# Expert weight ring with its xT slots last, p in a tile of its own, gate and up of the last 512 columns packed side by side, and a nested second fallback, in a two-layer decoder trunk

## The chip, the cores and the metric

The kernel runs on one core of one Trainium2 chip. The metric is device time in microseconds, the median of three runs. Five engines work side by side: TensorE (PE, its weight loads PEld), VectorE (DVE), ScalarE (ACT), GpSimd (POOL) and SyncE (SP); SP issues nearly all DMAs here, in order.

## The reference

A batch of one sequence of 256 tokens of width 1024 goes through two layers in float32. Layer 0 is forgetting and stick-breaking attention and a dense SwiGLU; layer 1 is sliding-window attention and a mixture of experts. What matters here is the mixture and what follows it:

```python
def moe_swiglu(x, router_w, router_b, w_gate_up, w_down):
    logits = jnp.einsum('td,de->te', xf, router_w) + router_b
    top_v, top_i = lax.top_k(logits, TOP_K)                    # 2 of 8 experts
    gates = jax.nn.softmax(top_v, axis=-1)
    ...
    for e in range(N_EXPERTS):                                 # swiglu: (silu(g) * u) @ w_down
        y = y + combine[:, e:e + 1] * swiglu(xf, w_gate_up[e], w_down[e])
...
x = layer_norm(DEEPNORM_ALPHA * x + h, ln_ffn_g[i], ln_ffn_b[i])
x = x + jax.nn.sigmoid(x @ ple_w_gate[i]) * (p[i] @ ple_w_proj[i])
```

An expert has 1024x3584 gate weights, as many up weights and 3584x1024 down weights. All eight are read: 336 tiles of 1 MiB.

## The kernel before

**Stages.** Layer 0 and the attention of layer 1 come first (up to about 464 us). Then come the router, the eight experts, and the end (layer norm, the gated embedding, the output). The experts run in an order sorted by their token counts, which the chip works out. GR gives each place in that order 3 or 2 groups of 32 tokens (3, 2, 3, 3, 2, 3, 3, 2). If some expert has more tokens than its place holds, a fallback runs all experts again for the rest: `experts(1, ...)`, and `experts(2, ...)` for still more. Both are compiled in, behind two tests one after the other (lines 1338 to 1341). With this input neither body runs.

**An expert.** An expert is cut in four quarters of the hidden width: 1024 columns three times, then 512. `gate_up(e, q)` multiplies the gathered tokens `xg` by gate and up weights. `trans(e, q)` transposes the product h, `down(e, q)` multiplies it by the down weights. The program goes gate_up(e, q), down of the quarter before, trans(e, q). `side_by_side` (line 1074) splits a weight row block in four strips and issues four matmuls for each group of 32 tokens, each into its own 32 PSUM partitions (a quarter of the array's columns). A T.matmul in float32 is two instructions in the trace.

For q below 3 the block is 1024 columns of gate, then 1024 of up, so the strips are 256 wide. For q = 3 the 1 MiB tile holds two k steps, each of 512 gate and 512 up columns. These are two blocks of 512 (lines 1096 and 1097), whose strips are 128 wide: as many matmuls as in another quarter, half as wide.

**The ring.** Weights go through 22 slots of 1 MiB, `ringtile` (line 787), in the cyclic order of TURNS (line 120). A digit or letter 0 to c is a slot of the ring pool, "p" one of 7 `raw` tiles, "x" one of two `xT` tiles. A tile's load waits until the tile 22 places before it has been read, and loads are issued in order (`fetch_`, line 830). The first AHEAD = 16 tiles, gate_up(0, 0) and gate_up(0, 1), are requested ahead of the router (line 853). The 17th to the 20th are the four of down(0, 0), then come those of gate_up(0, 2). In TURNS the two x stand at places 17 and 18, the slots 9, a, b, c after them.

The tag `xT` has two buffers. The router uses both for a transposed x (`xTf`, line 859). Then `pt1` (line 891), which holds p of layer 1 until `turn_p` (line 1211) has transposed it on TensorE, takes the first of them again, so the two x tiles get the second and, behind pt1, the first. `turn_p` is issued behind gate_up(0, 0) in the program; a scheduler sets each engine's static order.

**The end.** `Finish.load` and `Finish.prepare` take 21 further ring tiles after gate_up(7, 3): loads of 6 MiB, and weights split in high and low parts. down(7, 2), down(7, 3) and `Finish.end` follow.

Of the kernel before, what the change touches and what calls it, by code (L numbers as in the profile page):

```python
# [11 lines left out]
F32 = mybir.dt.float32  # L12
# [3 lines left out]
AF = mybir.ActivationFunctionType  # L16
ALU = mybir.AluOpType
AX = mybir.AxisListType

P = 128  # L20
S = 256
D = 1024
NB = S // P
# [14 lines left out]
CT = 32  # L38
# [36 lines left out]
def trunk(ctx: ExitStack, tc: tile.TileContext, cst, x, p, ln_mix_g, ln_mix_b, ln_ffn_g, ln_ffn_b, ab_w_in,  # L75
# [29 lines left out]
    V, A, T, G = (Engine(eng) for eng in (nc.vector, nc.scalar, nc.tensor, nc.gpsimd))  # L105

    def pool(name, bufs=1, **kw):
        return tc.tile_pool(name=name, bufs=bufs, **kw)

    cp = ctx.enter_context(pool("cp"))  # L110
    big = ctx.enter_context(pool("big"))
# [5 lines left out]
    HLW = 1024  # L117
    TMB = 1
    RB = 13
    TURNS = "3p4p5p6p7ppp2108xx9abc"  # L120
    KT = 2
    SC = (0, 2, 5)
    NLAST = (256, 256)
# [2 lines left out]
    def acc():  # L126
        return psA.tile([P, 512], F32, tag="acc", name="acc")

    def mis():
        return psM.tile([P, 512], F32, tag="mis", name="mis")  # L130
# [30 lines left out]
    ident = c[:, C_ID:C_ID + P]  # L161
# [16 lines left out]
    def gemm(hl, lhs, nk, w, col0, width, accs, seg=4, kh=2, korder=None, loaded=None, raws=None):  # L178
# [7 lines left out]
        for k0, kn in segs:  # L186
# [19 lines left out]
            for b in range(NB):  # L206
# [3 lines left out]
                for k in range(k0, k0 + kn):  # L210
                    H, L = parts[k]
                    for j, (a, W) in enumerate(((0, H), (0, L), (1, H))):
                        T.matmul(accs[b][:, :width], lhs(b, a, k), W,
                                 start=(k == 0 and j == 0), stop=(k == nk - 1 and j == 2))
# [13 lines left out]
    def tr4(src, n=4):  # L228
        ps = mis()
        for i in range(n):  # L230
            turned[0] = T.transpose(ps[:, i * P:(i + 1) * P], src[:, i * P:(i + 1) * P], ident)
        return ps

    def xTtile():
        return big.tile([P, 2, 8, P], F32R, tag="xT", name="xT", bufs=2)
# [12 lines left out]
    def lnp(g_ap, b_ap):  # L248
        g = big.tile([P, D], F32, tag="lng", name="lng", bufs=1)
        bt = big.tile([P, D], F32, tag="lnb", name="lnb", bufs=1)  # L250
        nc.sync.dma_start(g, g_ap.broadcast_to([P, D]))
        nc.sync.dma_start(bt, b_ap.broadcast_to([P, D]))
        return g, bt
# [65 lines left out]
    def to_xT(tiles):  # L319
        r = []  # L320
        for b in range(NB):
            t = xTtile()
            tsplit(tiles[b], t)
            r.append(t)
        return r
# [88 lines left out]
    xT = [xTtile()]  # L414
# [15 lines left out]
    with pool("hl0", 5, side="right") as hl, ExitStack() as es0:  # L430
# [160 lines left out]
        g, bt = lnp(ln_mix_g[0:1, :], ln_mix_b[0:1, :])  # L591
        order = [4, 5, 6, 7, 0, 1, 2, 3]
        accs = gemm_full(hl, lambda b, a, k: oT[:, a, order[k], b * P:(b + 1) * P], 8, ab_w_out[0], korder=order)
        xT = [xTtile() for b in range(NB)]
# [68 lines left out]
        with pool("ff", 1, reuse_waits="tile") as ff:  # L663
            hTs = []
            for f0 in range(0, DFF, 512):
                w = min(512, DFF - f0)
# [5 lines left out]
                hT = ff.tile([P, 2, 4, S], F32R, tag="hT", name="hT", bufs=6)  # L672
                hTs.append(hT)
                for b in range(NB):
                    h = ff.tile([P, 512], F32, tag="h", name="h", bufs=2)
# [3 lines left out]
            g, bt = lnp(ln_ffn_g[0:1, :], ln_ffn_b[0:1, :])  # L679
# [8 lines left out]
        with pool("pl", 1, reuse_waits="tile") as pl:  # L688
            xT = to_xT(xs)
# [7 lines left out]
        with pool("at1", 1, reuse_waits="tile") as at:  # L697
            xT = to_xT(xs)
# [27 lines left out]
            for b in range(NB):  # L726
# [6 lines left out]
                ps = tr4(kd.rearrange("p g r d -> p (g r d)"), 2)  # L733
# [38 lines left out]
            g, bt = lnp(ln_mix_g[1:2, :], ln_mix_b[1:2, :])  # L772
# [4 lines left out]
        moe = ctx.enter_context(pool("moe", 1, reuse_waits="tile"))  # L777
# [9 lines left out]
    def ringtile(dt=F32):  # L787

        i = TURNS[turn[0] % len(TURNS)]
        turn[0] += 1  # L790
        if i == "p":
            return rawtile(dt)
        if i == "x":
            return big.tile([P, 2048], dt, tag="xT", name="raw", bufs=2)
        return ring.tile([P, 2048], dt, tag="raw" + i, name="raw", bufs=1)
# [32 lines left out]
    chunks = [(c_.stop - c_.start) // P for c_ in cols]  # L828
# [24 lines left out]
    for i in range(AHEAD):  # L853
        t = ringtile()
# [3 lines left out]
    for b in range(NB):  # L858
        t = big.tile([P, 2, 8, P], F32, tag="xT", name="xTf", bufs=2)
        for k0 in range(0, 8, 4):  # L860
            ps = tr4(xs[b][:, k0 * P:(k0 + 4) * P])
            A.copy(t[:, 0, k0:k0 + 4, :], ps.rearrange("p (k t) -> p k t", t=P))
        ps = mis()
        for k in range(8):
            q = T.matmul(ps[0:NE, 0:P], rw[:, k, :], t[:, 0, k, :], start=(k == 0), stop=(k == 7))
# [3 lines left out]
    for b in range(NB):  # L869
        ps = lps[b]  # L870
# [13 lines left out]
        ps = mis()  # L884
# [3 lines left out]
        place_first(b)  # L888
        gather_first(b)

    pt1 = big.tile([P, NB, 256], F32, tag="xT", name="pt1", bufs=2)
    nc.sync.dma_start(pt1, p[1, 0].rearrange("(b p) n -> p b n", p=P))
    accx = xs

# [88 lines left out]
    def experts(rest, finish):  # L983

        st = {}
# [11 lines left out]
        used, passed = [0], [None]  # L997
# [24 lines left out]
        def weights(*it):  # L1022
            assert items[used[0]] == it
            used[0] += 1
            return fetch(*it)
# [47 lines left out]

        def side_by_side(out, lhs, W, first, last):

            w = W.shape[-1] // 4
            for g, (o, opens) in enumerate(out):
                for t in range(4):
                    mm = T.matmul(o[CT * t:CT * (t + 1), :w], lhs[g], W[:, w * t:w * (t + 1)],
                                  start=first and opens, stop=last, skip_group_check=True)  # L1080
            return mm

        def gate_up(e, q, hooks={}):
            xg = st[e]["xg"]
            n = gr[e]
            w = 32 * chunks[q]
            ac = [acc() for _ in range(n)]

            out = [[(ac[s][:, :w], True), (ac[s][:, w:2 * w], False)] + [(a[:, w * s:w * (s + 1)], s == 0) for a in ac[2:]]
                   for s in range(2)]  # L1090
            for k in range(8):
                lhs = [xg[:, k, CT * g:CT * (g + 1)] for g in range(n)]
                if q < 3:
                    W = [weights(e, q, k, s) for s in range(2)]
                else:
                    t = weights(e, q, k, 0)
                    W = [t[:, :512], t[:, 512:]]
                for s in range(2):
                    mm = side_by_side(out[s], lhs, W[s], k == 0, k == 7)
                if k in hooks:  # L1100
                    hooks[k](mm)
            h = moe.tile([P, 3 * 256], F32, tag="h", name="h", bufs=1)
            A.activation(h[:, :2 * w], ac[0][:, :2 * w], AF.Silu)
            V.tensor_tensor(h[:, :2 * w], h[:, :2 * w], ac[1][:, :2 * w], op=ALU.mult)
            if n > 2:
                A.activation(h[:, 2 * w:3 * w], ac[2][:, :w], AF.Silu)
                V.tensor_tensor(h[:, 2 * w:3 * w], h[:, 2 * w:3 * w], ac[2][:, w:2 * w], op=ALU.mult)
            st[e]["h%d" % q] = h

        def trans(e, q):  # L1110

            m = chunks[q] // 4
            n = gr[e] * m
            hT = moe.tile([P, 6, 4, CT], F32, tag="hT", name="hT", bufs=1)
            with tc.issue_after(passed[0].ins) if passed[0] else nullcontext():
                for i in range(0, n, 4):
                    j = min(4, n - i)
                    ps = tr4(st[e]["h%d" % q][:, i * P:(i + j) * P], j)
                    A.copy(hT[:, i:i + j].rearrange("p j t i -> p (j t i)"), ps[:, :j * P])
            st[e]["hT%d" % q] = hT  # L1120

        def down(e, q):
            n = gr[e]
            m = chunks[q] // 4
            if q == 0:
                st[e]["y"] = [mis() for _ in range((n + 1) // 2)]
            y = [(st[e]["y"][g // 2][:, 256 * (g % 2):256 * (g % 2 + 1)], g % 2 == 0) for g in range(n)]
            hT = st[e]["hT%d" % q]
            for k in range(chunks[q]):
                W = weights(e, q, k)  # L1130
                mm = side_by_side(y, [hT[:, g * m + k % m, k // m, :] for g in range(n)], W,
                                  q == 0 and k == 0, q == 3 and k == chunks[3] - 1)
                if k == min(KT, chunks[q] - 1):
                    passed[0] = mm
# [8 lines left out]
        def ystile():  # L1143
            return moe.tile([P, D], F32, tag="ys", name="ys", bufs=1)
# [38 lines left out]
        for e in range(NE):  # L1183
            for q in range(4):
# [17 lines left out]
                if e == NE - 1 and q == 3:  # L1202
                    scatter(e)[0](None)
        down(NE - 1, 3)
        ys = ystile()
        finish.end(functools.partial(collect, st[NE - 1]["y"], ys, gr[NE - 1]), ys, st[NE - 1]["pT"], CT * gr[NE - 1],
# [8 lines left out]
    class Finish:  # L1215
# [41 lines left out]
        def end(self, collect, ys, pT, c_, add):  # L1257
# [33 lines left out]
            with in_order():  # L1291
# [38 lines left out]
                for m in NLAST:  # L1330
# [3 lines left out]
                    c0 += m  # L1334

    experts(0, Finish())

    top = nc.values_load(cnti[0:1, 0:1], min_val=0, max_val=S + P)
    for rest in range(1, 3):
        with tc.If(top > P + 3 * CT * (rest - 1)):  # L1340
            experts(rest, Finish())


_INS = ['x', 'p', 'ln_mix_g', 'ln_mix_b', 'ln_ffn_g', 'ln_ffn_b', 'ab_w_in', 'ab_b_f', 'ab_w_out', 'c_w_qkv',
# [19 lines left out]
```

## Time and profile before

| what | value |
|---|---|
| median of 3 runs | 1430.46 us (1430.26 to 1434.83) |
| the profiled execution | 1428.27 us |
| its span, first to last instruction | 1426.5 us |
| TensorE busy | 1358.0 us (95%) |
| VectorE, ScalarE busy | 394.1 us, 325.2 us |
| moved by DMA | 434.03 MB, mean 304 GB/s |
| mean granted TensorE clock | 0.99 |

The profile is of one execution. Its span leaves out 1.77 us of its time. Ends of matmuls are modelled, so that a busy TensorE says little by itself; the duration of a phase is better read from its start to the start of the next.

### The profile page before, as it was taken

The numbers are of one execution on the slowest core, as the hardware profiler recorded it, in microseconds if no ns is written. First come the engines' busy times: TensorE is split into PE (matmuls) and PEld (weight loads), VectorE is DVE, ScalarE is ACT, GpSimd is POOL, SyncE is SP. The second block draws the span as 40 slices with busy tenths as digits, with TensorE's granted clock in tenths as the row PEclk, the third lists the DMA queues.
The fourth block names the chain that finished last, engine by engine and source line by source line (L and its number), as shares of the span: only waits on it lengthen the run. The fifth ranks groups of instructions, "written<-read, shape, count | busy, mean of one in ns | idle before, by whom it ended". The sixth has DMA issues, their size and how long they took to land. (4 is left out here: it accounts for less than half of the span.)

```text
span 1426.5 us, 40108 instructions
## 1 busy us (share of the span) xinstructions
PE 1358.0 (95%) x18290; PEld 927.4 (65%) x18290; DVE 394.1 (28%) x781; ACT 325.2 (23%) x618; POOL 27.5 (2%) x31
## 2 busy tenths in 40 slices
PE   8999899999999999898999899899999899999886
PEld 6786688887876666555556655665655665665545
DVE  5465755556676400010010010001010001001152
ACT  4545444434574101010010010010010001001131
POOL 0000200000000000000000000000000000000000
PEclk9999999999999999999999999999999999999988
DMA  9362553664573259999999999999999999999941
GB/s 323 142 209 78 185 178 118 206 207 166 204 287 118 98 223 401 407 408 401 407 408 391 406 408 391 403 408 396 396 408 403 390 408 407 387 406 407 359 186 35
DMA packets 143166, 434.03 MB, mean 304 GB/s; under 512 B 8834, under 2 KB 14978, under 8 KB 142978
## 3 DMA queue, kind: packets, MB, share of 16 engines
q1 hardware_dynamic: 142834, 431.22, 79.4%
q8 instruction: 147, 2.41, 0.7%
q14 instruction: 41, 0.34, 0.1%
q10 hardware_dynamic: 144, 0.07, 0.0%
HBM read 430.21 MB, written 1.05 MB: 302 GB/s over the span
## 5 line engine op out<-in xcount | busy, mean ns | idle before, releaser
L90 PE MATMUL acc<-raw,xg 128*32 128x256 f32 (+1 forms) x10752 | 528.5, 355 | 27.0 <-issue 23.1
L90 PEld LDWEIGHTS acc<-raw,xg 128*32 128x32 f32 x10752 | 333.4, 111 | 216.2 <-issue 41.0
L90 PE MATMUL mis<-raw,hT 128*32 128x256 f32 x4704 | 265.2, 379 | 7.1 <-DMA raw<-in_moe_w_down 4.0
L90 PE MATMUL acc<-H,xT 128*128 128x512 f32 (+2 forms) x768 | 226.1, 378 | 2.2 <-DVE xT L90 1.3
L90 PEld LDWEIGHTS mis<-raw,hT 128*32 128x32 f32 x4704 | 154.9, 110 | 107.4 <-issue 8.0
L90 DVE TENSOR_TENSOR h<-h,acc 128x512 f32<-128x512 f32 (+1 forms) x64 | 35.3, 552 | 681.3 <-PE acc L90 679.6
L90 DVE TENSOR_TENSOR L<-raw,H 128x1024 fp32r<-128x1024 f32 (+2 forms) x134 | 151.2, 1134 | 115.4 <-ACT H L90 114.7
L90 ACT CAST H<-raw 128x1024 fp32r<-128x1024 f32 (+2 forms) x138 | 133.6, 975 | 150.3 <-PE acc L90 144.3
L90 PEld LDWEIGHTS acc<-H,xT 128*128 128x128 f32 x768 | 139.4, 190 | 30.4 <-ACT xT L90 1.8
L90 ACT ACTIVATE h<-acc 128x512 f32<-128x512 f32 (+1 forms) x64 | 31.3, 489 | 515.0 <-PE acc L90 514.9
L90 PE MATMUL acc<-L,xT 128*128 128x512 f32 (+2 forms) x384 | 141.8, 375 | 0.0
L90 PEld LDWEIGHTS acc<-L,xT 128*128 128x128 f32 x384 | 72.7, 189 | 14.0 <-DVE L L90 1.2
L90 ACT COPY hT<-mis 128x512 f32<-128x512 f32 (+2 forms) x47 | 21.7, 495 | 202.2 <-PE mis L90 202.0
L90 PE MATMUL acc<-H,hT 128*128 128x512 f32 x176 | 55.8, 396 | 0.0
L90 DVE SCALAR_TENSOR_TENSOR x<-mis,gateT,x 128x512 f32<-128x512 f32 x28 | 21.0, 751 | 92.4 <-PE mis L90 90.9
L90 PE MATMUL acc<-H,oT 128*128 128x512 f32 x128 | 44.4, 413 | 0.0
L90 PEld LDWEIGHTS acc<-H,hT 128*128 128x128 f32 x176 | 33.0, 187 | 8.0
L90 PE MATMUL acc<-L,hT 128*128 128x512 f32 x88 | 34.8, 395 | 0.0
L90 DVE COPY ys<-mis 32x256 f32<-32x256 f32 x42 | 17.8, 423 | 49.9 <-ACT ys L90 42.0
L90 PEld LDWEIGHTS mis<-c,h 128*128 128x128 f32 x191 | 20.9, 140 | 13.6 <-issue 11.9
L90 PE MATMUL mis<-c,h 128*128 128x128 f32 x191 | 29.7, 281 | 0.0
L90 PEld LDWEIGHTS acc<-H,oT 128*128 128x128 f32 x128 | 24.0, 189 | 6.0 <-issue 0.8
(209 smaller groups left out, 792.2 us busy)
## 6 DMA issues: line engine op xcount, KB each, us to landing
raw<-in_moe_w_gate_up SPq DMA_DIRECT2D x192, 1024.0 KB, 18.4
raw<-in_moe_w_down SPq DMA_DIRECT2D x111, 1024.0 KB, 18.4
raw<-in_moe_w_gate_up SPq DMA_DIRECT2D x64, 512.0 KB, 13.3
raw<-in_ffn_w_gate_up SPq DMA_DIRECT2D x20, 1024.0 KB, 5.1
raw<-in_ffn_w_down SPq DMA_DIRECT2D x10, 1024.0 KB, 5.1
raw<-in_ab_w_in SPq DMA_DIRECT2D x9, 1024.0 KB, 8.0
raw<-in_ple_w_gate SPq DMA_DIRECT2D x8, 1024.0 KB, 13.3
raw<-in_ab_w_out SPq DMA_DIRECT2D x4, 1024.0 KB, 5.1
```

Of the source, the lines that this page charges most:

```text
L90: self.last = getattr(self.eng, name)(*args, **kw)
```

## The change

The last six places of TURNS are 8 9 a b c x x in place of 8 x x 9 a b c, so the x tiles become the 21st and 22nd. pt1 moves from `xT` to the `ys` tile of the pool moe, which is first needed otherwise when expert 0 is scattered back. For q = 3, `gate_up_last` takes the 1024 columns of gate and up of a k step as one block: strips of 256, the gate half into PSUM partitions 0 to 63, the up half into 64 to 127. SiLU and product then run on 64 partitions, and `trans` transposes 64-row pieces, twice as many. The second fallback stands inside the first, so that a program that skips the first meets one test.

```diff
-    TURNS = "3p4p5p6p7ppp2108xx9abc"
+    TURNS = "3p4p5p6p7ppp21089abcxx"
...
-    pt1 = big.tile([P, NB, 256], F32, tag="xT", name="pt1", bufs=2)
+    pt1 = moe.tile([P, D], F32, tag="ys", name="pt1", bufs=1)[:, :NB * 256].rearrange("p (b n) -> p b n", b=NB)
...
-            w = 32 * chunks[q]
+            if q == 3:
+                return gate_up_last(e, xg, n)
+            w = 256
...
-                if q < 3:
-                    W = [weights(e, q, k, s) for s in range(2)]
-                else:
-                    t = weights(e, q, k, 0)
-                    W = [t[:, :512], t[:, 512:]]
                 for s in range(2):
-                    mm = side_by_side(out[s], lhs, W[s], k == 0, k == 7)
+                    mm = side_by_side(out[s], lhs, weights(e, q, k, s), k == 0, k == 7)
...
+        def gate_up_last(e, xg, n):
+
+            ac = [acc() for _ in range((n + 1) // 2)]
+            out = [(ac[g // 2][:, 256 * (g % 2):256 * (g % 2 + 1)], g % 2 == 0) for g in range(n)]
+            for k in range(8):
+                side_by_side(out, [xg[:, k, CT * g:CT * (g + 1)] for g in range(n)], weights(e, 3, k, 0), k == 0, k == 7)
+            h = moe.tile([P, 3 * 256], F32, tag="h", name="h", bufs=1)
+            for i in range(0, n, 2):
+                m = 256 * min(2, n - i)
+                o = slice(256 * i, 256 * i + m)
+                A.activation(h[:64, o], ac[i // 2][:64, :m], AF.Silu)
+                V.tensor_tensor(h[:64, o], h[:64, o], ac[i // 2][64:, :m], op=ALU.mult)
+            st[e]["h3"] = h
+
         def trans(e, q):
 
-            m = chunks[q] // 4
+            m = 2
             n = gr[e] * m
             hT = moe.tile([P, 6, 4, CT], F32, tag="hT", name="hT", bufs=1)
+            if q == 3:
+                hT = hT.rearrange("p j t i -> p (j t i)")[:, :6 * 64].rearrange("p (j t i) -> p j t i", j=6, t=2)
+                ps = mis()
+                with tc.issue_after(passed[0].ins) if passed[0] else nullcontext():
+                    for i in range(n):
+                        T.transpose(ps[:, 64 * i:64 * (i + 1)], st[e]["h3"][:64, i * P:(i + 1) * P], ident[:64, :64])
+                    A.copy(hT[:, :n].rearrange("p j t i -> p (j t i)"), ps[:, :64 * n])
+                st[e]["hT3"] = hT
+                return
...
     top = nc.values_load(cnti[0:1, 0:1], min_val=0, max_val=S + P)
-    for rest in range(1, 3):
-        with tc.If(top > P + 3 * CT * (rest - 1)):
-            experts(rest, Finish())
+    with tc.If(top > P):
+        experts(1, Finish())
+        with tc.If(top > P + 3 * CT):
+            experts(2, Finish())
```

## Rows read from the trace of the kernel before

**Rows 1.** Windows: busy time of each engine, granted clock, DMA share, GB/s.

```profile
480.00:514.00 34.00, 34.00 (x621) 20.52 (x614) 1.93 (x7) 1.23 (x3) 0.00 (x0) 1.00 0.01 2
514.00:534.00 20.00, 20.00 (x354) 12.08 (x356) 1.11 (x2) 3.10 (x8) 0.00 (x0) 1.00 0.97 376
1160.00:1180.00 20.00, 20.00 (x366) 12.04 (x362) 2.59 (x6) 3.22 (x8) 0.00 (x0) 1.00 1.03 407
```

**Rows 2.** SP's own timeline, 472 to 515 us.

```profile
471.16 0.37 SPq L832 DMA_DIRECT2D raw<-in_moe_w_down  x1
513.97 1.39 SPq L832 DMA_DIRECT2D raw<-in_moe_w_down  x3
```

**Rows 3.** SP's waits, 466 to 516 us: total, times, longest.

```profile
SPq L832 <- PE mis L90: 45.7, 2, 41.7
```

**Rows 4.** Timeline around the router: start, duration, instruction, idle time before it.

```profile
463.22 0.39 PE L90 MATMUL acc<-H,oT 128*128 128x512 f32 x1
...
463.65 1.20 SPq L832 DMA_DIRECT2D raw<-in_moe_w_gate_up  x2
...
464.31 0.17 DVE L90 MEMSET lgT<- 64x128 f32 x1
...
469.18 1.91 PE L90 MATMUL mis<-xTf,rw 128*8 128x128 f32 x16
...
476.47 36.88 PE L90 MATMUL acc<-raw,xg 128*32 128x256 f32 x674
513.28 0.66 PE L90 MATMUL mis<-c,pt 128*128 128x128 f32 x4
```

**Rows 5.** Windows over the whole of experts 1, 3 and 4.

```profile
595.05:690.46 95.41, 91.13 (x1563) 53.95 (x1563) 8.03 (x14) 9.22 (x23) 2.70 (x4) 1.00 1.03 405
...
813.63:941.93 128.30, 123.88 (x2275) 79.18 (x2274) 9.58 (x18) 10.89 (x30) 0.00 (x0) 0.99 1.02 402
941.93:1026.94 85.01, 82.29 (x1531) 50.38 (x1534) 8.04 (x14) 7.12 (x17) 2.48 (x4) 1.00 1.02 398
```

**Rows 6.** TensorE's timeline, gate_up(0, 3) and what follows it.

```profile
566.07 0.87 PE L90 MATMUL mis<-c,h 128*128 128x128 f32 x6
566.87 4.55 PE L90 MATMUL acc<-raw,xg 128*32 128x128 f32 x155
573.01 3.70 PE L90 MATMUL acc<-raw,xg 128*32 128x128 f32 x128 [1.59 <-issue]
579.21 2.93 PE L90 MATMUL acc<-raw,xg 128*32 128x128 f32 x99 [2.50 <-issue]
581.87 0.44 PE L90 MATMUL mis<-raw,hT 128*32 128x256 f32 x2
...
594.57 0.55 PE L90 MATMUL mis<-c,h 128*128 128x128 f32 x3
...
743.27 10.54 PE L90 MATMUL mis<-raw,hT 128*32 128x256 f32 x192
```

**Rows 7.** The page: instruction counts of TensorE, and packets of the instruction queue.

```profile
PE 1358.0 (95%) x18290; PEld 927.4 (65%) x18290; DVE 394.1 (28%) x781; ACT 325.2 (23%) x618; POOL 27.5 (2%) x31
...
q8 instruction: 147, 2.41, 0.7%
```

**Rows 8.** Groups by shape, whole span: busy us, mean ns, idle before and its releasers.

```profile
L90 PE MATMUL acc<-raw,xg 128*32 128x256 f32 x8064 | 446.0, 380 | 3.9 <-DMA raw<-in_moe_w_gate_up 3.7
...
L90 PE MATMUL mis<-raw,hT 128*32 128x256 f32 x4704 | 265.2, 379 | 7.1 <-DMA raw<-in_moe_w_down 4.0 <-issue 3.0
...
L90 PE MATMUL acc<-raw,xg 128*32 128x128 f32 x2688 | 82.5, 280 | 23.1 <-issue 23.1
```

**Rows 9.** Line 1340, the tests: duration min/median/max in ns, first and last start.

```profile
L1340 SPq EVENT_SEMAPHORE  x16: 17/17/17, 1417.9 to 1425.1; - x16
...
L1340 SPq COMPARE_BRANCH  x2: 45/49/53, 1414.2 to 1421.0; - x2
```

**Rows 10.** Timeline of the end, from the last matmuls of down(7, 3).

```profile
1372.96 3.66 PE L90 MATMUL mis<-raw,hT 128*32 128x256 f32 x64 [0.72 <-DMA raw<-in_moe_w_down]
```

More of the change, by code (lines that the diff above doesn't have):

```diff
@@ L1123, in down @@
             n = gr[e]
-            m = chunks[q] // 4
+            m = 2
             if q == 0:
```

## Prediction

> **What bounds the kernel now.** I read the windows first, then SP's timeline and waits around the router, then TensorE's timeline through the experts, then the end. The reader is to see three things.
>
> First, a hole in the weight stream. From 480 to 514 us the DMA moves 2 GB/s; from 514 on it moves about 407 GB/s nearly all the way [rows 1]. SP issues the 17th tile at 471.16 us and the 18th to 20th from 513.97 us [rows 2]; its longest wait there is 41.7 us, for TensorE [rows 3]. The one thing of TensorE that ends there is `turn_p` on pt1, at 513.28 us [rows 4]. So the 18th tile, an x tile, waits for pt1's buffer, and all later loads stand behind it on SP.
>
> Second, the hole costs far less than its length. At 407 GB/s a tile takes 1.0486/0.407 = 2.58 us, an expert's 42 tiles 108 us. Expert 3 (three groups) takes TensorE 128.3 us, expert 4 (two groups) 85.0 us [rows 5]. So in an expert of three groups TensorE is the slower, and the ring (22 tiles, 57 us) fills; in one of two groups the stream is the slower, and the ring drains by about 23 us. Only expert 1 starves, since the ring was empty at 514.
>
> Third, gate_up(0, 3) doesn't run evenly: 128 matmuls take 3.70 us, then TensorE is idle for 2.50 us on "issue" [rows 6]. From 573.01 to 579.21 us is 6.20 us for 128 matmuls and as many weight loads. The instruction queue brought 147 packets for 36,580 instructions of TensorE, 249 in a packet [rows 7], so this reads as one packet of code each 6.2 us, in a stretch where half-wide matmuls use a packet up in 3.7 us. A full-width quarter uses one up in 128 x 55 ns = 7.0 us and shows no such gaps.
>
> From expert 2 to the end of expert 7 TensorE is therefore the bound, the code fetch in the eight last quarters included.
>
> **The change part by part.** All sums are in microseconds of the profiled execution.
>
> *Last quarter of gate and up.* Before, it is 2688 half-wide matmuls: 82.5 busy and 23.1 idle, 105.6 in all [rows 8]. After, it is 1344 full-width ones, in the shape that down already uses. The full-width row of gate_up has 446.0 + 3.9 over 8064, or 55.8 ns each [rows 8], so 1344 take 75.0: a saving of 30.6. The bounds: a down phase of 192 takes 10.54, 54.9 ns each [rows 6], which gives 31.8; the down row with all its idle time has 272.3 over 4704, 57.9 ns [rows 8], which gives 27.8. I take 30.6, the same operand tiles.
>
> *The down behind it.* down(0, 2) runs from 581.87 to 594.57, 12.7 for what elsewhere takes 10.54 [rows 6]: it still pays for code that is behind. Four other experts are late there by 0.9, 0.3, 1.1 and 0.7, by the same reading, 5.1 with this one. Idle time on "issue" is 3.0 of it [rows 8]. With the halved rate of instructions the fetch isn't behind. I take 5, from 3 to 5.
>
> *The transposes.* Quarter 3 transposes twice as many pieces, of 64 columns. The six of a full quarter take 0.87, the three of quarter 3 take 0.55 [rows 6], so at most 0.32 more with three groups and about 0.22 with two: 5 x 0.32 + 3 x 0.22 = 2.3 lost. From below, half-wide pieces could cost nothing more. I take 2.
>
> *SiLU and product* run on 512 columns of 64 partitions in place of 256 of 128. They come behind gate_up(e, 3) and their result is read only after down(e, 2), over 7 later, which hides them. Without that cover they would cost some 0.5 an expert. In expert 7 ScalarE's splits for the end queue behind the SiLU; 0.2 lost.
>
> *The ring and pt1.* After the change the 17th to 20th tiles go to 9, a, b, c, over space whose last reader is the output projection, ended at 463.6; the 21st and 22nd to the two xT buffers, whose last reader is the router's second product, ended at 471.1 [rows 4]. pt1's load goes to a pool whose space was written from 464.31 on [rows 4], so nothing holds it up on SP either. So the 22 tiles are on their way by 472, and the 23rd needs only the first step of gate_up(0, 0), at 476.47 + 2.6. The stream has no hole. What this gives is the starving of experts 1 and 2: idle on weight loads it is 3.7 [rows 8] and 4.0, of which 2.3 lie in the end, so 5.4; but stretched matmuls hide some. Expert 1 takes 95.4, expert 4 with the same work 85.0 [rows 5]; expert 1 gathers for two experts besides, about 5.0. That leaves 5.4, and the first quarter of expert 2 is 2 late. I take 7, from 5.4 to 7.5.
>
> Is the stream fast enough for the faster TensorE? An expert of three groups now takes 128 - 7 = 121 against 108, one of two groups 83 to 88 against 108. The ring starts full at 57, falls to some 32 in expert 1, is full again in expert 3, and meets expert 7 full. It never runs dry, so the saved 34 of TensorE come through.
>
> *The nested test.* Skipping a test, SP branches at 1414.2, works off eight semaphores up to 1420.9, branches again at 1421.0, and is through at 1425.1 [rows 9]. The second test alone is 4.2, branch to last semaphore. The first took 6.8; if the one that remains runs as short as the second, 6.8 goes. I take 4.2, from 3.6 to 6.8. It can't be hidden: nothing else runs behind 1421.
>
> Sum: 30.6 + 5 - 2 - 0.2 + 7 + 4.2 = 44.6. From 1428.27 this leaves 1383.7. The profiled execution lay 2.2 below the median of the runs, so the median comes to 1386. With all lower ends it is 27.8 + 3 - 2.3 - 0.5 + 5.4 + 3.6 = 37.0, with all upper ends 31.8 + 5 + 7.5 + 6.8 = 51.1: 1379 to 1393.
>
> **The rivals.**
>
> *The hole stays* (something else holds the 17th to 22nd tile until 514). Then TensorE runs into the stream: 319 expert tiles and 6 of the end are to come after 514, 325 x 2.58 = 838, so the last lands at 1352, and its matmuls end at about 1354 in place of 1376.6 [rows 10]: 22 saved, with the test 27, or 1404. For it: TURNS has been one chain, and one late slot stops everything behind it. Against it: the last readers above, all before 472.
>
> *The gaps aren't code fetch.* The Trainium skill, "Runtime: NRT & Kernel Launch", section "Instruction fetch mechanics", says that crossing a block of code is mostly hidden, since the sequencer dispatches more slowly than blocks arrive. As a mechanism of this kernel: the 23.1 of idle time would stay, and only the per-matmul cost would shrink. Two half-wide ones take 2 x 82.5/2688 = 61.4 ns, one full-width one 446.0/8064 = 55.3 ns [rows 8]; 1344 x 6.1 ns = 8.2. The sum is 8.2 - 2 + 7 + 4.2 = 17, or 1413. The trace speaks against that rule here: gaps come once in 128 matmuls, at 6.20 us, in the half-wide quarter alone [rows 6].
>
> *The end swallows it.* The last down loads wait for ring slots that the end's splits set free. If they stood fixed in time, TensorE would wait there. But these slots are freed by work that starts behind gate_up(7, 3), so they move with it. Price at most what the first rival says.
>
> *Slower.* SP is held by pt1's load or an x tile longer than now. Each microsecond past 514 costs one, on top of 1404, so it takes a hold until 545 to be slower by over 0.3%. For it: pt1 shares its new tile with the scatter of expert 0, and the scheduler may put `turn_p` elsewhere. Against it: no x tile has pt1 ahead of it any more.
>
> **How the numbers follow.** The forecast has 0.79. The hole staying (or the end swallowing it) has 0.10, the gaps staying 0.06, slower 0.03; the remaining 0.02 is for gains that come to nothing. 0.3% is 4.3 us, about what a measurement of this kernel can tell from no change. All but the last two are faster: 0.95; same 0.02, slower 0.03. The range goes from 1376, somewhat under the sum of all upper ends, to 1404, where the first rival lies; it leaves out the others and some of that one, under 0.2.
>
> **What would show it.** Right: DMA near 400 GB/s from 480 to 514; no wait of TensorE for weights in experts 1 and 2; gate_up(e, 3) in 10.5 with three groups and 7.0 with two, without "issue" before its matmuls; one SP branch of the test and some 4 to 7 less behind the last store. Wrong: a wait of over 10 on SP behind the 16th tile; TensorE waiting for weights in expert 7, which would mean that the stream is now the bound; full-width matmuls with gaps as before.

## The result and the profile after

The changed kernel takes 1380.7 us (median of 4 runs, 1380.06 to 1381.38), beside 1431.71 for the kernel before, measured with it: a ratio of 0.9641, 95% interval 0.9622 to 0.966. Forecast were 1386 and a range of 1376 to 1404. The profiled execution took 1380.5 us, its span 1378.7; before they were 1428.27 and 1426.5.

The windows of the changed kernel, in the columns of [rows 1]: the hole, then two of the old stretches.

```profile
480.00:514.00 34.00, 34.00 (x630) 20.35 (x622) 2.79 (x13) 0.98 (x2) 0.28 (x1) 1.00 1.02 406
514.00:534.00 20.00, 20.00 (x344) 12.28 (x346) 1.11 (x2) 3.35 (x8) 0.00 (x0) 1.00 1.04 396
1160.00:1180.00 20.00, 20.00 (x344) 11.40 (x340) 2.61 (x4) 0.98 (x2) 0.00 (x0) 1.00 0.98 378
```

Where the DMA moved 2 GB/s [rows 1], it now moves 406. SP's waits from 466 to 516 us (total, times, longest) have nothing left of the 41.7 us of [rows 3]:

```profile
SPq L832 <- PE acc L90: 30.8, 14, 7.5
SPq L832 <- PE mis L90: 2.1, 1, 2.1
```

TensorE's timeline of the changed kernel at the last quarter of expert 0 and the end of expert 7 answers to [rows 6]:

```profile
567.76 10.57 PE L90 MATMUL acc<-raw,xg 128*32 128x256 f32 x192
578.15 10.54 PE L90 MATMUL mis<-raw,hT 128*32 128x256 f32 x192
588.62 0.58 PE L90 MATMUL mis<-c,h 64*128 64x64 f32 x6
...
1302.39 7.09 PE L90 MATMUL acc<-raw,xg 128*32 128x256 f32 x128
```

gate_up(0, 3) is one unbroken run of 192 matmuls, with no "issue" idle before any of them; from its start to that of down(0, 2) it takes 10.4 us, before 15.0. The page's counts and the groups by shape say the same for all eight experts [rows 7, 8]:

```profile
PE 1350.3 (98%) x16967; PEld 896.7 (65%) x16967; DVE 396.3 (29%) x781; ACT 326.5 (24%) x618; POOL 27.4 (2%) x31
...
q8 instruction: 135, 2.21, 0.7%
```

```profile
L90 PE MATMUL acc<-raw,xg 128*32 128x256 f32 x9408 | 519.7, 380 | 0.0
L90 PE MATMUL mis<-raw,hT 128*32 128x256 f32 x4704 | 262.7, 379 | 1.4 <-DMA raw<-in_moe_w_down 1.4
```

The 9408 are the old 8064 and 1344 new ones. Their idle time is 0.0, where the two old groups had 3.9 and 23.1. Behind the last store one test is left, at line 1359 (operation, count, duration in ns, first and last start):

```profile
L1359 SPq EVENT_SEMAPHORE  x8: 17/17/17, 1376.7 to 1377.2; - x8
...
L1359 SPq COMPARE_BRANCH  x1: 53/53/53, 1373.6 to 1373.6; - x1
```

**Where the 47.8 us went.** By the starts and ends of phases in TensorE's timelines of the two kernels:

| stretch | before | after | gain |
|---|---|---|---|
| first matmul to start of gate_up(0, 0) | 476.5 | 477.4 | -0.9 |
| gate_up(e, 3) to down(e, 2), e 0 to 6; gate_up(7, 3) itself | 99.5 + 8.9 | 71.6 + 7.1 | 29.7 |
| down(e, 2) and trans(e, 3), e 0 to 6 | 84.1 | 78.9 | 5.2 |
| experts 1 and 2 elsewhere (weights late before) | | | 7.4 |
| end of gate_up(7, 3) to end of down(7, 3) | 25.8 | 25.0 | 0.8 |
| from there to the last matmul | 35.8 | 37.3 | -1.5 |
| last matmul to the end of the span | 14.1 | 6.9 | 7.2 |

The second to fourth lines make the eight experts 832.1 long in place of 874.4. By windows over the whole of three of them, against [rows 5]:

```profile
589.20:679.20 90.00, 89.09 (x1441) 51.77 (x1444) 8.30 (x14) 9.29 (x23) 2.68 (x4) 1.00 1.03 403
794.50:916.10 121.60, 121.60 (x2085) 73.32 (x2084) 9.90 (x18) 11.25 (x30) 0.00 (x0) 1.00 1.02 402
916.10:997.90 81.80, 81.80 (x1406) 47.42 (x1408) 8.30 (x14) 7.25 (x16) 2.46 (x4) 1.00 1.03 402
```

### The profile page after: what moved, and what is told of

Its sections match the earlier page's. It is cut to its first block, busy times and chain, and to the rows that moved or that the text cites. A ratio compares the mean times of both kernels' runs of the same rounds, so it can differ in the third digit from the quotient of the medians.

```text
span 1378.7 us, 37452 instructions
## 1 busy us (share of the span) xinstructions
PE 1350.3 (98%) x16967; PEld 896.7 (65%) x16967; DVE 396.3 (29%) x781; ACT 326.5 (24%) x618; POOL 27.4 (2%) x31
## 5 line engine op out<-in xcount | busy, mean ns | idle before, releaser
L90 PE MATMUL acc<-raw,xg 128*32 128x256 f32 x9408 | 519.7, 380 | 0.0
L90 PEld LDWEIGHTS acc<-raw,xg 128*32 128x32 f32 x9408 | 300.9, 110 | 209.7 <-issue 11.3
L90 DVE TENSOR_TENSOR h<-h,acc 128x512 f32<-128x512 f32 (+2 forms) x64 | 37.7, 596 | 638.1 <-PE acc L90 479.0
L90 PEld LDWEIGHTS mis<-raw,hT 128*32 128x32 f32 x4704 | 151.8, 110 | 103.0 <-DMA raw<-in_moe_w_down 2.1
L90 ACT ACTIVATE h<-acc 128x512 f32<-128x512 f32 (+2 forms) x64 | 32.9, 522 | 481.7 <-PE acc L90 481.7
L90 DVE COPY ys<-mis 32x256 f32<-32x256 f32 x42 | 17.8, 423 | 47.8 <-ACT ys L90 40.6
L90 PEld LDWEIGHTS mis<-c,h 128*128 128x128 f32 (+1 forms) x212 | 21.7, 140 | 14.0 <-issue 12.3
L90 PE MATMUL mis<-c,h 128*128 128x128 f32 (+1 forms) x212 | 30.1, 271 | 0.0
## 6 DMA issues: line engine op xcount, KB each, us to landing
raw<-in_moe_w_gate_up SPq DMA_DIRECT2D x192, 1024.0 KB, 18.1
```

The source lines that it names most:

```text
L90: self.last = getattr(self.eng, name)(*args, **kw)
```

## The experiments

**Theories.** *Additive:* TensorE is the bound from expert 2 on, the stream has room, and so each part gives its own term: the quarter some 34, ring and pt1 7, the test 4 or more. *Rival: two bounds.* The stream is close behind TensorE, so that the quarter alone runs into it, and a stream mended alone runs into the quarter. Also open were what the gaps in the last quarter are, which half of "ring and pt1" does the work, and why the end gained 7.2 and not 4.2.

**1. Ring and pt1 alone** (ring_only: the kernel before, with two lines changed).

```diff
-    TURNS = "3p4p5p6p7ppp2108xx9abc"
+    TURNS = "3p4p5p6p7ppp21089abcxx"
-    pt1 = big.tile([P, NB, 256], F32, tag="xT", name="pt1", bufs=2)
+    pt1 = moe.tile([P, D], F32, tag="ys", name="pt1", bufs=1)[:, :NB * 256].rearrange("p (b n) -> p b n", b=NB)
```

> The kernel before with the new ring order and pt1 in the ys tile; the last quarter and the two tests as before. Theory (the hole only starves experts 1 and 2): the DMA runs through from 480 to 514 us, the waits of TensorE for weights in experts 1 and 2 vanish, the span falls by 7 (5.4 to 7.5). Rival (the whole hole is on the path): it falls by 35 or more. Rival (nothing): within 2.

Measured: 1416.11 us, ratio 0.9884 (0.9866 to 0.9901), 15.6 under the median before. That lies between the theories, and in the trace for two reasons. Experts 1 and 2 are 5.5 and 2.2 shorter: that is the term of 7. Expert 0 is 4.1 shorter besides, and there the windows and TensorE's timeline of this kernel show something not foreseen:

```profile
514.00:600.00 86.00, 84.01 (x1647) 58.14 (x1641) 2.93 (x6) 9.30 (x21) 0.00 (x0) 1.00 1.00 381
```

```profile
569.46 4.55 PE L90 MATMUL acc<-raw,xg 128*32 128x128 f32 x155
575.70 3.70 PE L90 MATMUL acc<-raw,xg 128*32 128x128 f32 x128 [1.69 <-issue]
579.70 2.93 PE L90 MATMUL acc<-raw,xg 128*32 128x128 f32 x99 [0.31 <-issue]
```

The last-quarter code is that of before, but its second gap is 0.31 in place of 2.50 [rows 6]. The DMA, with the ring nearly full, moves 381 GB/s over this stretch, and 225 and 215 in the windows from 576 to 578 and 578 to 580 us, where that gap lies. So the gaps go with the stream; experiment 6 takes that up.

**2. The last quarter alone** (q3_only: the kernel before with gate_up_last and the new trans).

```diff
+            if q == 3:
+                return gate_up_last(e, xg, n)
```

> The kernel before with the last quarter in two array halves alone; ring, pt1 and tests as before. Theory (the hole stays, so a faster TensorE runs into the stream): gate_up(e, 3) falls to 10.5 and 7.0 us as in the changed kernel, some 34 in all, but TensorE waits for weights for some 20 in place of 7, in experts 1, 5 and 7, and the span falls by only 21 to 24. Rival (the parts simply add up): it falls by 33 to 36. Rival (the gaps are not for code): by 6 to 8, with the gaps still there.

Measured: 1428.55 us, ratio 0.9975 (0.9964 to 0.9986): 3.2 gained. All three expectations were too high. TensorE's waits (total, times, longest) and one window over nearly all of the experts:

```profile
PE mis L90 <- DMA raw<-in_moe_w_down: 14.1, 19, 2.0
PE acc L90 <- DMA raw<-in_moe_w_gate_up: 11.1, 22, 1.9
PE mis L90 <- ACT raw L90: 9.3, 1, 9.3
```

```profile
514.00:1340.00 826.00, 802.45 (x13608) 467.76 (x13596) 65.39 (x115) 71.84 (x172) 7.60 (x12) 1.00 1.02 400
```

All last quarters run as in the changed kernel where weights are there, but experts 1, 4 and 7 take 102.5, 92.0 and 81.6 in place of 90.0, 81.8 and 74.6, and the stretch to the end of down(7, 3) 31.7 in place of 25.0. TensorE waits for weights while the DMA is busy throughout (share 1.02). That is the rival, plainer than it was stated: with the hole, the stream was the bound as soon as TensorE got faster. The whole hole is then paid for. It lasts from 479 to 518 us here (DMA windows of 2 us), and beside the changed kernel, which has none, the eight experts take 33.4 longer (865.6) and the stretch behind them 6.7: 40 for a hole of 39.

**3. The nested test alone** (nested_only).

```diff
-    for rest in range(1, 3):
-        with tc.If(top > P + 3 * CT * (rest - 1)):
-            experts(rest, Finish())
+    with tc.If(top > P):
+        experts(1, Finish())
+        with tc.If(top > P + 3 * CT):
+            experts(2, Finish())
```

> The kernel before with the second fallback inside the first and nothing else. Theory (the changed kernel's trace): from the last matmul to the end of the span 6.8 us in place of 14.05, the span falls by 7. Rival (my forecast's term): by 4.2. Nothing ahead of the last store changes.

Measured: 1425.16 us, ratio 0.9953 (0.9936 to 0.9969), 6.6 gained. From the last matmul to the end of the span 6.6 us are left of 14.1. SP's rows of the test in this kernel:

```profile
L1339 SPq EVENT_SEMAPHORE  x8: 17/17/17, 1418.5 to 1419.1; - x8
...
L1339 SPq COMPARE_BRANCH  x1: 53/53/53, 1415.6 to 1415.6; - x1
```

From branch to last semaphore the one test takes 3.5. Of the two of before, the first took 6.8 and the second 4.2 [rows 9], so by these rows it is the first one's time that goes. That time isn't a fixed price: by the same reading the first of two took 3.8, 6.4 and 5.3 in the kernels of experiments 1, 2 and 6, the second 4.1, 3.7 and 3.2. Why it varies stays open.

The three alone add up to 3.2 + 15.6 + 6.6 = 25.4; together they give 51. So some 26 us are there only when quarter and stream are mended at once (if the test adds its 6.6 either way; quarter and stream without the test were not run).

**4 and 5. Which half mends the stream** (the changed kernel, with the old TURNS; the changed kernel, with pt1 back in xT).

```diff
-    TURNS = "3p4p5p6p7ppp21089abcxx"
+    TURNS = "3p4p5p6p7ppp2108xx9abc"
```

> The changed kernel with the ring order of before (x tiles at places 17 and 18); pt1 stays in the ys tile. Theory A (pt1's tile alone made the hole): no hole, the same time as the changed kernel within 2. Theory B (the order matters too): a hole again behind the 16th tile and some 10 to 13 slower than the changed kernel.

```diff
-    pt1 = moe.tile([P, D], F32, tag="ys", name="pt1", bufs=1)[:, :NB * 256].rearrange("p (b n) -> p b n", b=NB)
+    pt1 = big.tile([P, NB, 256], F32, tag="xT", name="pt1", bufs=2)
```

> The changed kernel with pt1 back in the xT tile; the new ring order stays. The second x tile, now the 22nd of the ring, must wait for the transposes of p at 514 us. Theory (what counts is how far the stream is ahead when it stops): the stream stops behind the 21st tile, from about 483 to 514 us, TensorE waits for weights in expert 1 for about 10, and the kernel is 8 to 11 us slower than the changed one. Rival (the order alone is enough): same as the changed kernel within 2.

Measured: old order 1381.38 us, ratio 0.9643 (0.9629 to 0.9657), the same as the changed kernel, with all eight experts within 0.1 of its. pt1 back: 1411.7, ratio 0.9853 (0.9836 to 0.987), 31 slower than the changed kernel. Windows of the latter, and SP's longest wait from 466 to 530 us:

```profile
489.00:517.00 28.00, 28.00 (x521) 16.83 (x514) 1.11 (x2) 0.98 (x2) 0.00 (x0) 1.00 0.01 4
520.00:600.00 80.00, 80.00 (x1420) 49.30 (x1416) 3.25 (x6) 7.99 (x17) 0.00 (x0) 1.00 1.03 404
600.00:1300.00 700.00, 687.14 (x11656) 401.51 (x11650) 61.45 (x108) 60.64 (x148) 7.64 (x12) 1.00 1.02 403
```

```profile
SPq L832 <- PE mis L90: 53.1, 3, 41.9
```

With the x slots last the ring gets four tiles further before it meets pt1, and no more: a hole of some 29 us stays (490 to 519 us by DMA windows of 2 us), and all of it is paid, in experts 1, 2, 4, 5 and 7 and at the end (2.6, 1.8, 10.3, 2.0, 6.7 and 6.7). pt1's own tile is what counts. With it, the new order gives nothing that these runs can tell; without it, the order only shortens the hole, from 39 us to 29.

**6. The gaps without a stream** (no_stream: the kernel before; experts 3 to 5 load no weights, but for the last down tiles of expert 5, and multiply by what lies in ring tiles).

```diff
+            if not rest and 3 <= e <= 5 and (e, q, s) != (5, 3, None):
+                ...
+                    raws[2] = next(again)
+                return raws[2][:, FQ * s:FQ * (s + 1)]
```

> The kernel before, in which experts 3 to 5 load no weights and read 13 tiles of the ring that are already there (so their products are not those of the reference). TensorE's instructions are the same. Theory (code comes late because its packets share the DMA engines with the weight stream): in gate_up(3, 3), (4, 3) and (5, 3) the gaps on issue shrink or vanish, 128 half-wide matmuls and the gap behind them take 3.7 to 4.5 us in place of 6.2, and three-group quarters 11 to 12 us in place of 15 to 17. Rival (the sequencer itself is that slow, whatever the DMA does): the gaps stay, 6.2 us per 128.

Measured, one run: 1405.07 us. Its TensorE timeline in gate_up(0, 3), beside the stream, and in gate_up(3, 3), where the window shows 3 GB/s:

```profile
566.88 4.55 PE L90 MATMUL acc<-raw,xg 128*32 128x128 f32 x155
573.25 3.70 PE L90 MATMUL acc<-raw,xg 128*32 128x128 f32 x128 [1.82 <-issue]
579.45 2.93 PE L90 MATMUL acc<-raw,xg 128*32 128x128 f32 x99 [2.50 <-issue]
...
906.66 10.69 PE L90 MATMUL acc<-raw,xg 128*32 128x128 f32 x384
```

```profile
560.00:600.00 40.00, 34.07 (x789) 24.16 (x785) 0.71 (x2) 2.00 (x5) 0.00 (x0) 1.00 1.03 405
900.00:930.00 30.00, 30.00 (x711) 22.91 (x704) 0.71 (x2) 2.01 (x6) 0.00 (x0) 1.00 0.01 3
```

The same 384 half-wide matmuls take 10.69 us in one piece when the DMA is idle, and 15.6 with gaps when it moves 405 GB/s. gate_up(3, 3) falls from 17.1 in the kernel before to 10.7, gate_up(4, 3) from 9.1 to 7.2, gate_up(5, 3) from 15.4 to 11.3. Half-wide matmuls are no dearer than full-width ones (10.57 us for the same multiplications). That the gaps are late code, the packets of the instruction queue show. Over the two stretches (566.88 to 582.49 and 906.66 to 917.35 us) they are (count, MB, share of 16 engines):

```profile
q8 instruction: 2, 0.03, 0.9%
...
q8 instruction: 3, 0.05, 2.1%
```

Beside the stream these packets of 16 KiB start 6.2 us apart, at 570.77, 576.97 and 583.17 us (the trace's own records of DMA packets), and each of the three gaps around gate_up(0, 3) and down(0, 2) ends 2.4 to 2.5 us after one. Without the stream they start at 907.78, 911.40 and 915.16, 3.6 to 3.8 apart, and there are no gaps. A packet itself takes 1.1 to 1.2 us in both; what holds it back before it starts the trace doesn't show. The Trainium skill, "Runtime: NRT & Kernel Launch", section "Instruction fetch mechanics", has a block's crossing mostly hidden: the idle stretch agrees, the stretch beside the stream (5 us lost in a quarter) doesn't.

**7. No test at all** (no_fallback: the changed kernel without tests and fallback bodies).

```diff
-    top = nc.values_load(cnti[0:1, 0:1], min_val=0, max_val=S + P)
-    with tc.If(top > P):
-        experts(1, Finish())
-        with tc.If(top > P + 3 * CT):
-            experts(2, Finish())
```

> The changed kernel without the fallback: neither test nor bodies (for tokens beyond the places it would leave them out; with this input none are). It prices the one test that is left. Theory (the test's branch costs 3.0 us of SP and its semaphores 0.6, the landing of the last store hides under it): the span falls by 1 to 4. Rival (a test costs 7, as the second one did): by 6 to 7.

Measured: 1378.92 us, ratio 0.9631 (0.9614 to 0.9647), 1.8 under the changed kernel, which these medians don't tell from no change; in the profiled executions the time from the last matmul to the end of the span falls from 6.9 to 4.1. By that the last test costs some 2 to 3 us, less than half of the one taken away.

**8 to 10. The end in another order** (end_reordered, the changed kernel run again beside it, end_on_dve). The end of the changed kernel waits for weights of down(7, 2) and down(7, 3), then for ScalarE, and then runs at 1.2 GHz from 1337 to 1351 us (granted clock 0.51 in that window). TensorE's timeline there:

```profile
1328.22 1.93 PE L90 MATMUL mis<-raw,hT 128*32 128x256 f32 x32 [0.30 <-DMA raw<-in_moe_w_down]
1330.86 3.66 PE L90 MATMUL mis<-raw,hT 128*32 128x256 f32 x64 [0.70 <-DMA raw<-in_moe_w_down]
1337.02 7.15 PE L90 MATMUL acc<-ys,pTe 64*128 64x512 f32 x8 [2.50 <-ACT ys L90]
```

The edit requests the last down tiles of expert 7 ahead of the end's own weights, prepares p earlier, and puts half of the later splits behind down(7, 3), their low parts on GpSimd; the last version puts these on VectorE.

```diff
+                if e == NE - 1 and q == 2:
+                    finish.load_p()
-                    finish.load()
+                    hasten(e, 2)
+                    hasten(e, 3)
...
+                for H, L, src in self.later:
+                    V.tensor_tensor(L, src, H, op=ALU.subtract)
```

> The changed kernel with its end in another order: the weights and splits of p ahead of gate_up(7, 3), the last six down tiles requested ahead of the end's own weights, and half of the end's splits behind the collecting copies, their low parts on GpSimd. Theory (the idle 3.85 us behind gate_up(7, 3) waits for ScalarE's splits, and the 1.45 us inside the last downs for loads that stand behind the end's): both vanish and the kernel is 4 to 6 us faster than the changed one. Rival (the stream is the bound at the end): the weights of the end land later and TensorE waits for them instead; no gain, within 2.

> The changed kernel once more, beside the reordered end: 1380 to 1382.

> This is the changed kernel with the preparation of p ahead of gate_up(7,3), the last six weight tiles of down(7) requested ahead of the end's own weights, and half of the later splits done late, as in the reordered end, but with the low parts of those late splits on VectorE behind the first one, and none on GpSimd. Theory (VectorE's norm steps took 5.6 us rather than 1.4 because GpSimd worked on two 1024-wide subtractions beside them): the norm's two steps fall back to below 2 us, the stretch from the end of down(7,3) to the last matmul is 4 to 7 us shorter than in the reordered end, and the time is 1376 to 1379, 2 to 5 under the changed kernel's. Rival (the last stretch waits for its late weights and runs at half the clock whatever VectorE does): the norm's steps stay above 4 us or TensorE waits for a load there, and the time is within 2 of the changed kernel's.

Measured: end_reordered 1383.56 us, ratio 0.9673 (0.9652 to 0.9694); the changed kernel again 1380.86, 0.9655 (0.9633 to 0.9676); end_on_dve 1380.08, 0.9637 (0.9624 to 0.965). No gain in either. Timeline of end_reordered:

```profile
1337.91 1.42 DVE L90 SCALAR_TENSOR_TENSOR raw<-x,mv,raw 128x512 f32<-128x512 f32 x2
...
1339.06 5.22 POOL L90 TENSOR_TENSOR raw<-raw 128x1024 fp32r<-128x1024 f32 x2
1339.24 5.58 DVE L90 SCALAR_TENSOR_TENSOR raw<-raw,rs 128x512 f32<-128x512 f32 x2
...
1342.13 1.12 PE L90 MATMUL mis<-c,raw 128*128 128x128 f32 x4 [4.35 <-DVE raw L90]
```

And of end_on_dve, at the same place:

```profile
1342.14 1.41 DVE L90 SCALAR_TENSOR_TENSOR raw<-raw,rs 128x512 f32<-128x512 f32 x2
...
1342.93 1.97 PE L90 MATMUL mis<-c,raw 128*128 128x128 f32 x8 [2.12 <-DVE raw L90]
```

The step of the norm fell back from 5.58 to 1.41, as the theory of VectorE held up by GpSimd says; but the kernel won nothing that can be told from the changed one, as the rival says. In both versions down(7, 3) ends 12 us sooner behind gate_up(7, 3) (13.1 for 25.0), expert 7, which now holds p's products, is 5.8 longer, and the stretch to the last matmul is 43.3 and 38.9 in place of 37.3. In end_on_dve TensorE needs 889.9 from gate_up(0, 0) to the last matmul, beside 894.5 and 892.9 in the two executions of the changed kernel: at most a gain of 3 to 5 that the medians don't bear out.

## Why the prediction was right, and where it was not

In the main the mechanism was right: the hole went, the last quarter runs without gaps, the test got shorter. Term by term, in microseconds of the profiled execution:

| step | forecast | measured |
|---|---|---|
| last quarter | 30.6 | 29.7 |
| down behind it, transposes, SiLU | 5 - 2 - 0.2 | 5.2 in all |
| ring and pt1 (experts 1 and 2) | 7 | 7.4 |
| nested test | 4.2 | 7.2 |
| not foreseen: start and end | 0 | -1.6 |
| sum | 44.6 | 47.9 |

**Last quarter.** Size and cause hold. That the gaps are late code was argued from 6.20 us a packet [rows 6, 7]; experiment 6 bears it out, packet by packet, and shows besides that they go with the stream. The forecast took 6.2 us a packet as fixed and didn't ask about that.

**Transposes.** Mis-sized: six 64-row pieces take 0.58 us where three of 128 took 0.55 [rows 6], 0.03 more and not up to 0.32. The forecast priced a piece by the row of full-size ones; smaller pieces are cheaper.

**Nested test.** Mis-sized: of the two tests the first cost 6.8 and the second 4.2 [rows 9], and the one that remains is as short as the second, 3.6. So the first one's price goes. The prediction named this case and took the lower figure.

**Ring and pt1.** The 7 are right as what experts 1 and 2 gain, and wrong as what the edit is worth beside the other two. With pt1 back in xT the changed kernel loses 31, where the forecast's own rival made it 18 (1404 less 1386). What the prediction had wrong is the room of the stream, "is full again in expert 3, and meets expert 7 full". It took 121 us, the time of expert 3, for every expert of three groups, and 108 for the stream's share, from 407 GB/s, though its own windows over whole experts show 398 to 405 [rows 5]. Measured are 111.8, 115.3, 121.6, 119.9 and 117.1 with three groups and 90.0, 81.8 and 74.6 with two, 832.1 together, and 401 GB/s over the whole stretch (window of the changed kernel from 480 to 1300 us, DMA share 1.02):

```profile
480.00:1300.00 820.00, 819.09 (x14084) 485.97 (x14080) 68.15 (x128) 72.24 (x173) 7.89 (x13) 1.00 1.02 401
```

So the stream needs 42 x 1.0486 / 0.401 = 109.8 an expert, 879 for eight, 46 more than TensorE. Counted in the trace, as bytes landed less tiles read, the ring's lead is some 50 us at the end of expert 3, near full, but 37 where expert 7 starts and 11 at the end of gate_up(7, 3). A tile takes 18.1 us from its issue to its landing besides (the page's list of DMA issues, median). The changed kernel gets through without a wait for weights until the last downs, where it waits 1.4. Such a wait in expert 7 is what the prediction named as the sign that the stream is now the bound, and by this count the two bounds all but meet there. "It never runs dry" held by a margin much thinner than the text gave it, and luck has a part in that.

**The rival of the hole.** It was priced at 1404, with the range ending there; experiment 5, whose hole is some 10 us shorter, measured 1411.7. The working set the last landing at 1352 and the end of down(7, 3) at 1354; with the old hole (experiment 2) down(7, 3) ends at 1376.1. Of these 22 us, 325 tiles at 400 in place of 407 GB/s are 325 x 1.0486 x (1/0.400 - 1/0.407) = 15. Some 4 more are the hole's end, at 518 us in that execution and not at 514. The rest lies in the end and was not told apart.

**From the profile to the median.** The forecast added 2.2 because the profiled execution of before lay below the median shown. In the result it lay 3.4 below the median before, and that of the changed kernel 0.2 below its own. So 3.2 of the 51 us between the medians are such an offset. It goes with the granted clock: of the executions of the kernel before that were timed beside the experiments, the four under 1429 us list a mean clock of 0.989 or 0.990, as the profiled one does, and all others 0.980 to 0.987. Part of it lies ahead of the experts. From 100 to 120 us the granted clock is 1.00, 0.91, 0.83 or 0.77 to 0.78, by execution, and gate_up(0, 0) starts at 476.2 to 476.5, 477.4 to 477.6, 478.9 to 479.7 or 480.2 to 480.5 us in the same order. The -0.9 in the first line of the table of stretches is of this kind (1.00 before, 0.91 after). Why the clock falls there in some executions and not in others stays open.

## What to carry to other kernels

Before a wait of the engine that sets the end is credited with a gain, add up the second resource over the same stretch, with every stage's own length and the rate that the windows show over hundreds of microseconds: here 832 of TensorE stood beside 879 of the stream, and either mending alone gave 3 and 16 us where both gave some 44 (51 less the test's 6.6). A buffer lent to a value that lives longer than the ring's turn (pt1) stops every load issued behind it; give it space of its own before reordering slots. Halving the number of TensorE's instructions for the same multiplications gained almost nothing here with the DMA idle (10.57 for 10.69 us) and 5 us a quarter beside the weight stream, so look for gaps on "issue" where a stream runs.

## What the runs showed of the hardware

- Code arrived late under a saturated stream: 384 half-wide matmuls took 15.6 us at 405 GB/s, with a code packet each 6.2 us, and 10.69 at 3 GB/s, with one each 3.6 to 3.8, in the same execution.
- Two VectorE steps on two SBUF inputs took 5.58 us beside two GpSimd subtractions of 1024 columns, 1.41 without them. The Trainium skill, "SBUF — State Buffer", section "SBUF: two separate sides", has a VectorE step with two SBUF inputs and a GpSimd step that reads SBUF exclude each other for the whole instruction; the two rows, which end within 0.6 us of each other, agree.
- Of two skipped tests in a row at the end of the program, the first took 3.8 to 6.8 us from SP's branch to SP's next one, by execution; passing one test in place of two gained 6.6. The last costs 2 to 3 by the profiled executions with and without it.
